# Moving the weights' buffers by 192 bytes in SBUF, and another w_ada item on TensorE

## The chip, the cores and the metric

The kernel runs on one core of a Trainium2 chip, in float32 (float32r for the large products). The metric is the device time in microseconds (us) of one execution; lower is better. Engines are named as the profile names them: PE is TensorE's matmul, PEld its load of the stationary operand, DVE is VectorE, ACT ScalarE, POOL GpSimd, SP SyncE, which issues most DMAs.

## The reference, cut to what matters

One layer of a streaming encoder over 256 frames of 2048 channels: a modulation from the vector c, a token mixer (gated linear attention beside a short convolution), and a convolutional feed-forward part.

```python
mod = silu(c) @ w_ada + b_ada                      # 2048 -> 6 * 2048
sh1, sc1, g1, sh2, sc2, g2 = split(mod, 6)
h = rmsnorm(x, norm_g[0]) * (1 + sc1) + sh1
y = token_mixer(h, w_in, ...)                      # h @ w_in, then w_out_gla, w_out_conv, w_o
x = x + g1 * rmsnorm(y, norm_g[1])
h = rmsnorm(x, norm_g[2]) * (1 + sc2) + sh2
gate, up = split(h @ w_up, 2)                      # 2048 -> 2 * 5632
y = (gelu(causal_dwconv(gate)) * up) @ w_down      # 5632 -> 2048
x = x + g2 * rmsnorm(y, norm_g[3])
```

Every weight is read once from HBM; the weights are most of the 363 MB that the profile counts.

## The kernel before, in words

**Three products for one.** The kernel splits each large operand into a float32r part and the rest: weights into `whi` and `wlo`, activations into a high and a low part. A product is the sum of high x high, high x low and low x high, three matmuls of float32r.

**A stream of chunks.** All weights pass as chunks of two blocks of 128 rows by 512 columns. For a chunk, SP issues a DMA into a buffer of the tag `raw` (nine buffers), ACT casts it into `whi` (L283), DVE subtracts it into `wlo` (L292), four buffers each, and TensorE does its matmuls. One list, `stream`, holds the order of all chunks, and `pump` walks it: DMAs are issued up to 13 chunks ahead, splits 4 ahead. `Feat` chunks (L339) put the weights' block in the array as the stationary operand and stream 256 columns of activations past it; `Tok` chunks (L394) hold 128 frames of the activations and stream 512 columns of weights.

**The places in SBUF.** One pool gives every tag its buffers in the order in which the tags are first named, so the size of one tile moves all tags behind it. The tile `H` holds the activations' two parts, 16 rows of `H_ROW` = 576 floats: the low part in columns 0 to 255, the high part from column 256 (with two more columns at one point). A row is 2304 bytes, nine times 256. Adding up the sizes, a tile's start modulo 256 bytes, its place, is

| tags | place |
|---|---|
| activations: `H` (all rows, both parts), `B`, `g8` | 64 |
| `t1` | 64 |
| `XF`, `t2` | 32 |
| `raw`, `c4`, `whi`, `wlo`, `A`, `cb` (behind `H`) | 0 |

Buffers of one tag and the blocks within them lie whole multiples of 256 bytes apart. Behind the 16 rows `H` has 32 unused floats.

**The start.** The first two of the six parts of the modulation (sh1, sc1) are needed before h exists. They are computed in five slices of channels (`SLICES`); the first covers 256 channels. For it w_ada comes in eight items, `Ada(0, 0)` to `Ada(0, 7)`, each two blocks of 128 rows in one `raw` buffer, two DMAs of 256 KB (L458). An item is added on DVE (L469 for the first block, L472 for the others: multiply by silu(c), add) or, if it stands in `ON_PE`, multiplied on TensorE (L229: the raw weights as stationary operand, one column of silu(c) streaming; a float32 matmul shows as two records). After the last item's turn DVE's sum is folded over partitions (L209 transposes, L211 adds) and `make_h` lets TensorE add the fold to the slice's bank (L217), from which DVE and ACT make scale and shift (L248, L249) and the first columns of H (L254 and following). The first L339 matmul needs these and the first `whi`.

```python
def split(self):                       # of Ada
    for t in range(self.nk):
        if (s, self.i) in ON_PE:
            break
        ...                            # one addition on DVE
    if self.last:
        acc_s[s] = fold(...)
def mm(self):
    if (s, self.i) in ON_PE:
        for t in range(self.nk):
            sum_cols(s, self.raw[:, :, t, :], sil[:, self.k0 + t:self.k0 + t + 1])
    if self.last:
        ...                            # make_h(s)
```

TensorE takes its work in the order of the stream, item by item.

Of the kernel before, what the change touches and what calls it, by code (L numbers as in the profile page):

```python
# [9 lines left out]
F32R = mybir.dt.float32r  # L10
# [5 lines left out]
P = 128  # L16
T = 256
D = 2048
KD = D // P
H = 4  # L20
# [7 lines left out]
TAU = 16.0  # L28
KT = 2
H_ROW = 576  # L30
NC = 512


# [21 lines left out]
MID0, MID = 2, 4  # L55
SQ0, SQ1 = 3, 4
EARLY_G = [1, 0, 6, 13]
ON_PE = {(0, 5)}


@with_exitstack
def hybrid_layer(ctx, tc, x, c, w_ada, b_ada, norm_g, w_in, w_a2, b_a2, gla_norm_g,
# [7 lines left out]
    def sb(shape, tag, bufs=1, dt=F32):  # L70
        count[0] += 1
        return pool.tile(list(shape), dt, tag=tag, bufs=bufs, name=f"{tag}_{count[0]}")
# [98 lines left out]
    for s in range(2):  # L171
        for q in range(2):
            ps = mm_banks()
            for a in range(8):
                k = 8 * q + a
# [13 lines left out]

    def moving():  # L190

        t = sb([P, KD * H_ROW + 32], "H", 1, F32R)[:, 0:KD * H_ROW].rearrange("p (k n) -> p k n", k=KD)
        return t[:, :, T:], t[:, :, 0:T]

    h_hi, h_lo = moving()
    mod1 = sb([P, 2, KD], "mod1")
    bmod1 = sb([P, 2, KD], "bmod1")
# [66 lines left out]
    class Chunk:  # L264
# [9 lines left out]
        def dma(self):  # L274
            g = self.g
            self.raw = sb([P, KT, NC], "raw", RAW_BUFS)[:, 0:self.n, :]
            r = g.row0 + self.k0 * P
            nc.sync.dma_start(
                self.raw, g.w[r:r + self.n * P, g.n0:g.n0 + NC].rearrange("(t p) n -> p t n", p=P))

        def split(self):
            self.hi = sb([P, KT, NC], "whi", SPLIT_BUFS, F32R)[:, 0:self.n, :]
            nc.scalar.copy(self.hi, self.raw)  # L283
            self.lo = sb([P, KT, NC], "wlo", SPLIT_BUFS, F32R)[:, 0:self.n, :]
            if pos[2] < first_w:
                first_lo.append(self.split_lo)
            else:
                self.split_lo()
# [154 lines left out]
    class Ada:  # L443
# [17 lines left out]
        def split(self):  # L461
            s = self.s
# [3 lines that stand above are left out]
# [14 lines left out]
        def mm(self):  # L480
            s = self.s
            if (s, self.i) in ON_PE:
                for t in range(self.nk):
# [322 lines left out]
    def post_ya(g):  # L806
        def post(j, v):
            if not m_t:
                m_t["hi"], m_t["lo"] = moving()
            k = 4 * g + j  # L810
            t = tiles(t2())
            nc.vector.tensor_mul(t, v, ga_t["t"][:, k:k + 2, :])
            nc.vector.tensor_add(t, t, gb_t["t"][:, k:k + 2, :])
            split_pair(m_t["hi"][:, k:k + 2, 0:T], m_t["lo"][:, k:k + 2, :], t)
        return post
# [326 lines left out]
    with tc.high_priority():  # L1142
        xs["hi"], xs["lo"] = moving()
        nc.vector.tensor_copy(xs["hi"][:, :, T], sh2)
        nc.vector.tensor_sub(xs["hi"][:, :, T + 1], sh2, f(xs["hi"][:, :, T]))
        for q in range(4):
            n = slice(512 * q, 512 * (q + 1))
            for s in range(2):
                def x1():
                    return nc.vector.scalar_tensor_tensor(  # L1150
                        xin["t"][:, s, n], y_t["t"][:, s, n], r1[:, s:s + 1], xin["t"][:, s, n],
                        op0=ALU.mult, op1=ALU.add).ins
                if len(mid) == 3:
                    with tc.issue_after(mid[2]):
                        x1()
                else:
                    ins = x1()
                    if s == 1:
                        mid.append(ins)
            for k in range(4 * q, 4 * q + 4, 2):  # L1160
                ps = sm_bank()
                for a in range(2):
                    for s in range(2):
                        nc.tensor.transpose(ps[:, a * T + s * P:a * T + (s + 1) * P],  # L1164
                                            xin["t"][:, s, (k + a) * P:(k + a + 1) * P], ident)
                for a in range(2):
                    sc, v = s2[:, k + a:k + a + 1], ps[:, a * T:(a + 1) * T]
                    hi = xs["hi"][:, k + a, 0:T]
                    mid_act.append(nc.scalar.mul(hi, v, sc).ins)
                    nc.vector.scalar_tensor_tensor(xs["lo"][:, k + a, :], v, sc, f(hi),  # L1170
                                                   op0=ALU.mult, op1=ALU.subtract)
# [63 lines left out]
```

## Time and profile before

| | |
|---|---|
| median of 3 runs | 1451.68 us (1450.31 to 1453.68) |
| the profiled execution | 1453.29 us |
| its span, first to last instruction | 1451.5 us |
| mean granted clock of TensorE | 0.994 |
| busy: PE, PEld, DVE, ACT | 98%, 92%, 71%, 55% |
| HBM read | 363.18 MB, 252 GB/s over the span |

The profile shows one execution. A row of the costliest groups reads: line, engine, operation, output <- inputs, their shapes, count, then busy time in us, mean duration in ns, and the engine's idle time ahead of it with what ended it. Matmuls overlap in the pipeline, so their duration (about 280 ns) is not what one costs; the distance of their starts is. A row of the chain or of the timeline begins with start and length in us. Tile names stand without their numbers (`t` for t1 and t2, `c` for c4, `g` for g8).

### The profile page before, as it was taken

How to read it: one execution, taken by the hardware profiler on the slowest of the kernel's cores; microseconds unless marked ns; L12 is line 12 of the kernel's file. 1: busy time of each engine (PE TensorE's matmuls, PEld its weight loads, DVE VectorE, ACT ScalarE, POOL GpSimd, SP SyncE). 2: the span in 40 equal slices, each digit the busy share in tenths (PEclk: the TensorE clock that was granted, in tenths of full speed). 3: DMA queues.
4: the chain of work that ended last, by engine and by line, in shares of the span. 5: the costliest groups of instructions: out<-in, count | busy, mean ns of one | idle time of the engine just before them, and what ended most of it. 6: DMA issues, size and time to landing. Idle time of an engine off the chain costs nothing.

```text
span 1451.5 us, 25558 instructions
## 1 busy us (share of the span) xinstructions
PE 1425.8 (98%) x10385; PEld 1336.3 (92%) x10385; DVE 1036.6 (71%) x1153; ACT 792.9 (55%) x952; POOL 7.1 (0%) x28
## 2 busy tenths in 40 slices
PE   6999999999999999999999999999999999999997
PEld 6999999899999999887999998789999988999986
DVE  6887878889988877975897666656666644555554
ACT  5788777689554655444764444344444433444443
POOL 0000000000000000000000000000000000000000
PEclk9999999999999999999999999999999999999999
DMA  9999989989988778886568777677776666666651
GB/s 353 366 339 310 375 286 360 328 288 331 372 285 280 245 251 317 304 299 183 151 199 264 238 234 235 231 239 236 230 228 204 200 188 190 187 184 185 186 174 59
DMA packets 178095, 366.97 MB, mean 253 GB/s; under 512 B 14026, under 2 KB 26648, under 8 KB 177209
## 3 DMA queue, kind: packets, MB, share of 16 engines
q1 hardware_dynamic: 176857, 362.17, 75.4%
q0 software_dynamic: 544, 2.11, 0.4%
q8 instruction: 81, 1.33, 0.4%
q10 hardware_dynamic: 576, 1.05, 0.2%
q14 instruction: 37, 0.30, 0.1%
HBM read 363.18 MB, written 2.11 MB: 252 GB/s over the span
## 4 chain that ended last, share of the span: by engine, by line
PE 93%; DVE 3%; DMA 2%; ACT 1%; issue 1%; SPq 0%; DVEq 0%; ACTq 0%
PE mm L339 63%; PE mm L394 28%; DMA raw<-in_w_ada_dram 2%; DMA XF<-in_x_dram 1%; DVE wlo L292 0%; DVE c L432 0%; DMA raw<-in_w_in_dram 0%; PE sm L1164 0%; SPq L458 0%; ACT whi L283 0%; DVE t L789 0%; PE sm L773 0%; DVE fold L211 0%; DVE c L472 0%; PE sm L217 0%
## 5 line engine op out<-in xcount | busy, mean ns | idle before, releaser
L283 ACT CAST whi<-raw 128x1024 fp32r<-128x1024 f32 (+1 forms) x503 | 512.6, 1024 | 525.3 <-PE mm L339 280.4
L292 DVE TENSOR_TENSOR wlo<-raw,whi 128x1024 fp32r<-128x1024 f32 (+1 forms) x503 | 595.4, 1191 | 285.5 <-ACT whi L283 275.7
L339 PE MATMUL mm<-H,whi 128*128 128x256 f32 (+1 forms) x4992 | 649.3, 281 | 1.6 <-ACT H L254 1.2
L339 PEld LDWEIGHTS mm<-H,whi 128*128 128x128 f32 x4992 | 616.1, 189 | 3.9 <-ACT H L254 1.3
L339 PE MATMUL mm<-H,wlo 128*128 128x256 f32 (+1 forms) x2496 | 350.2, 280 | 0.0
L339 PEld LDWEIGHTS mm<-H,wlo 128*128 128x128 f32 x2496 | 318.5, 188 | 0.0
L394 PE MATMUL mm<-whi,g 128*128 128x512 f32 x704 | 181.5, 395 | 0.0
L394 PEld LDWEIGHTS mm<-whi,g 128*128 128x128 f32 x704 | 131.9, 188 | 31.7
L432 DVE SCALAR_TENSOR_TENSOR c<-raw,sil,c 128x1024 f32<-128x1024 f32 x90 | 115.2, 1280 | 35.7 <-DMA raw<-in_w_ada_dram 35.6
L394 PE MATMUL mm<-whi,H 128*128 128x512 f32 x448 | 118.5, 396 | 0.0
L394 PEld LDWEIGHTS mm<-whi,H 128*128 128x128 f32 x448 | 83.5, 188 | 19.6
L394 PE MATMUL mm<-wlo,g 128*128 128x512 f32 x352 | 99.3, 395 | 0.0
L394 PEld LDWEIGHTS mm<-wlo,g 128*128 128x128 f32 x352 | 66.1, 188 | 16.0
L472 DVE SCALAR_TENSOR_TENSOR c<-raw,sil,c 128x768 f32<-128x768 f32 (+2 forms) x73 | 78.6, 1077 | 2.0 <-DMA raw<-in_w_ada_dram 1.4
L394 PE MATMUL mm<-wlo,H 128*128 128x512 f32 x224 | 65.7, 395 | 0.0
L432 DVE SCALAR_TENSOR_TENSOR cb<-raw,sil,cb 128x1024 f32<-128x1024 f32 x30 | 38.5, 1284 | 24.7 <-DMA raw<-in_w_ada_dram 24.7
L394 PEld LDWEIGHTS mm<-wlo,H 128*128 128x128 f32 x224 | 42.1, 188 | 10.2
L982 DVE SCALAR_TENSOR_TENSOR t<-mm,fcol,t 128x255 f32<-128x255 f32 x80 | 38.4, 480 | 1.2
L339 PE MATMUL mm<-B,whi 128*128 128x256 f32 x256 | 33.5, 282 | 0.0
L339 PE MATMUL mm<-g,whi 128*128 128x256 f32 x256 | 32.8, 280 | 0.0
L339 PEld LDWEIGHTS mm<-B,whi 128*128 128x128 f32 x256 | 31.4, 188 | 1.4 <-ACT t L712 0.8
L339 PEld LDWEIGHTS mm<-g,whi 128*128 128x128 f32 x256 | 31.3, 188 | 0.0
(193 smaller groups left out, 687.1 us busy)
## 6 DMA issues: line engine op xcount, KB each, us to landing
raw<-in_w_up_dram SPq DMA_DIRECT2D x176, 512.0 KB, 4.3
raw<-in_w_ada_dram SPq DMA_DIRECT2D x160, 512.0 KB, 5.2
raw<-in_w_in_dram SPq DMA_DIRECT2D x145, 512.0 KB, 5.8
raw<-in_w_down_dram SPq DMA_DIRECT2D x88, 512.0 KB, 3.8
raw<-in_w_o_dram SPq DMA_DIRECT2D x32, 512.0 KB, 5.6
raw<-in_w_ada_dram SPq DMA_DIRECT2D x32, 384.0 KB, 6.1
raw<-in_w_out_conv_dram SPq DMA_DIRECT2D x16, 512.0 KB, 6.1
raw<-in_w_out_gla_dram SPq DMA_DIRECT2D x16, 512.0 KB, 5.4
```

Of the source, the lines that this page charges most:

```text
L283: nc.scalar.copy(self.hi, self.raw)
L292: nc.vector.tensor_sub(self.lo, self.raw, f(self.hi))
L339: nc.tensor.matmul(dst[:, 0:cols], w[:, t, j * P:(j + 1) * P], m(ch.k0 + t, cols), start=first_in_bank and t == 0 and i == 0, stop=end and ...
L394: nc.tensor.matmul(self.out[s], m(c.k0 + t, T)[:, s * P:(s + 1) * P], w[:, t, :], start=first and t == 0 and i == 0, stop=end and t == c.n ...
L432: nc.vector.scalar_tensor_tensor(a, self.raw, sil[:, self.k:self.k + 1], a, op0=ALU.mult, op1=ALU.add)
L472: nc.vector.scalar_tensor_tensor(a, raw, sc, a, op0=ALU.mult, op1=ALU.add)
L982: nc.vector.scalar_tensor_tensor(dst[:, a, i:], v[:, a, 0:T - i], w(2 - i, a), dst[:, a, i:], op0=ALU.mult, op1=ALU.add)
```

## The change

Two edits. `H` is allocated with 80 unused floats instead of 32 behind its rows, and its use still begins at its first float (`H_AT` = 0). All tags behind it move by 192 bytes, so that `raw`, `c4`, `whi`, `wlo`, `A` and `cb` begin at place 192 of 256; `H`, `B` and `g8` stay at 64. And of the first slice's items TensorE takes the last, number 7, instead of number 5; DVE adds items 0 to 6.

```diff
 H_ROW = 576
+H_AT, H_PAD = 0, 80
 NC = 512
...
-ON_PE = {(0, 5)}
+ON_PE = {(0, 7)}
...
     def moving():
 
-        t = sb([P, KD * H_ROW + 32], "H", 1, F32R)[:, 0:KD * H_ROW].rearrange("p (k n) -> p k n", k=KD)
+        t = sb([P, KD * H_ROW + H_PAD], "H", 1, F32R)[:, H_AT:H_AT + KD * H_ROW]
+        t = t.rearrange("p (k n) -> p k n", k=KD)
         return t[:, :, T:], t[:, :, 0:T]
```

## Prediction

> **What bounds the kernel now.** I read the page's busy times and slices first, then the chain of waits, then short windows, because the change moves operands of nearly every matmul and I wanted the matmul's rhythm stage by stage.
>
> ```profile
> span 1451.5 us, 25558 instructions
> PE 1425.8 (98%) x10385; PEld 1336.3 (92%) x10385; DVE 1036.6 (71%) x1153; ACT 792.9 (55%) x952; POOL 7.1 (0%) x28
> PE   6999999999999999999999999999999999999997
> PE 93%; DVE 3%; DMA 2%; ACT 1%; issue 1%; SPq 0%; DVEq 0%; ACTq 0%
> L283 ACT CAST whi<-raw 128x1024 fp32r<-128x1024 f32 (+1 forms) x503 | 512.6, 1024 | 525.3 <-PE mm L339 280.4
> ```
>
> TensorE is busy from the second slice to the last, holds 93% of the chain that ended last, and the cast that makes whi waits mostly for TensorE to give a buffer back. So TensorE sets the pace and the others follow it. What a matmul costs from start to start is read off the chain's long uninterrupted pieces:
>
> ```profile
> 763.66 115.81 PE mm L339 x981
> 969.44 144.16 PE mm L339 x1224
> 1150.72 89.60 PE mm L394 x384
> 1240.32 135.68 PE mm L339 x1152
> ```
>
> With a moving operand of 256 columns (L339) that is 144.16 / 1224 = 117.8 ns, and 135.68 / 1152 = 117.8 ns; with 512 columns (L394) 89.60 / 384 = 233.3 ns. The piece of 981 gives 118.1. These are constant over stages with different loads on DVE, ACT and the DMAs.
>
> ```profile
> L339 PE MATMUL mm<-H,whi 128*128 128x256 f32 (+1 forms) x4992 | 649.3, 281 | 1.6 <-ACT H L254 1.2
> L339 PE MATMUL mm<-H,wlo 128*128 128x256 f32 (+1 forms) x2496 | 350.2, 280 | 0.0
> L339 PE MATMUL mm<-B,whi 128*128 128x256 f32 x256 | 33.5, 282 | 0.0
> L339 PE MATMUL mm<-g,whi 128*128 128x256 f32 x256 | 32.8, 280 | 0.0
> L394 PE MATMUL mm<-whi,g 128*128 128x512 f32 x704 | 181.5, 395 | 0.0
> L394 PE MATMUL mm<-whi,H 128*128 128x512 f32 x448 | 118.5, 396 | 0.0
> L394 PE MATMUL mm<-wlo,g 128*128 128x512 f32 x352 | 99.3, 395 | 0.0
> L394 PE MATMUL mm<-wlo,H 128*128 128x512 f32 x224 | 65.7, 395 | 0.0
> ```
>
> That is 8000 matmuls at 117.8 ns (942 us) and 1728 at 233.3 ns (403 us): 1345 of 1451.5 us hang on two rhythms. One nanosecond on the first is 8 us.
>
> **Edit 1, the places.** The longer H moves every tile named after it by 192 bytes: raw, c4, whi, wlo, A and cb from place 0 to 192 of 256. H, B and g8, the activations, stay at 64. No instruction and no byte of traffic is added. The question is whether the rhythm depends on the distance between the operand that streams and the one that is loaded, which goes from 64 to 128. No row of the trace has a whi or wlo at another distance, so its price is bounded.
>
> For an effect: there is a second rhythm at the same places.
>
> ```profile
> 25.00:31.00 6.00, 5.66 (x25) 5.47 (x26) 5.95 (x9) 3.61 (x5) 0.00 (x0) 0.50 1.06 399
> 68.40:70.90 2.50, 2.50 (x24) 2.50 (x23) 2.11 (x4) 2.50 (x6) 0.00 (x0) 1.00 0.94 329
> 744.00:763.00 19.00, 19.00 (x170) 19.00 (x170) 19.00 (x35) 12.65 (x17) 0.00 (x0) 1.00 0.65 187
> 800.00:850.00 50.00, 50.00 (x427) 50.00 (x426) 32.48 (x34) 22.18 (x26) 0.00 (x0) 1.00 0.75 237
> ```
>
> These are windows: start and end, length, then busy time and count of PE, PEld, DVE, ACT and POOL, granted clock, DMA share, GB/s. A matmul of 280 ns overlaps its neighbours, so a window counts 280 / 117.8 = 2.4 too many. From 800 to 850 that is 50.00 / (427 - 2.4) = 117.8 ns. From 744 to 763 it is 19.00 / (170 - 2.4) = 113.4 ns, at full clock, with the same operands, and with DVE fully busy. So up to 4.4 ns of the 117.8 are a matter of how streams meet in time.
>
> Against an effect: the weights' load is not what costs them.
>
> ```profile
> 397.82 0.19 PEld L339 LDWEIGHTS mm<-B,wlo 128*128 128x128 f32 x1
> 397.94 0.11 PEld L694 LDWEIGHTS sm<-H,t 128*32 128x32 f32 x1
> 398.05 0.28 PE L694 MATMUL sm<-H,t 128*32 128x256 f32 x1
> 398.99 0.28 PE L339 MATMUL mm<-B,whi 128*128 128x256 f32 x1
> ```
>
> Between 398.05 and 398.99 stand eight matmuls with weights of only 32 or 16 columns (tile t, place 32 or 160, so at distances that whi never has). Their load takes 0.11 us instead of 0.19, and yet they come every 0.94 / 8 = 117.5 ns. A quarter or an eighth of the weights read, at other distances, and the rhythm is the same. Also, during one L339 matmul the moving operand runs through 256 columns of 4 bytes while 128 columns of weights are read: 1024 against 512 bytes. The distance between the two therefore sweeps 512 bytes, two whole turns of 256, wherever it starts; in L394 it is 2048 against 512. A start at 128 instead of 64 changes when they meet, not how often. And 512 columns cost 233.3 / 117.8 = 1.98 times 256, although only one load of weights lies beside either: the cost goes with the moving columns. I take 0 for edit 1, by the L694 rows, which are the nearest to another distance; the ends are the quick rhythm everywhere and, by symmetry, the same 4.4 ns lost.
>
> The DMAs now write raw at place 192, where a row of 2 KB touches nine blocks of 256 bytes instead of eight.
>
> ```profile
> 4.00:9.00 5.00, 0.00 (x0) 0.00 (x0) 0.00 (x0) 3.13 (x6) 0.00 (x0) 1.00 1.00 399
> 25.00:62.00 37.00, 36.66 (x251) 34.88 (x252) 32.97 (x35) 25.27 (x27) 0.00 (x0) 0.91 1.05 393
> 100.00:300.00 200.00, 199.92 (x1524) 189.94 (x1523) 162.92 (x160) 151.76 (x172) 0.00 (x0) 1.00 0.94 331
> ```
>
> From 4 to 9 us the traffic is mostly x into XF, which lies at place 32: 399 GB/s at a share of 1.00. From 25 to 62 raw is written at place 0: 393 GB/s at 1.05. A destination off the 256-byte line is no slower, so I count nothing. The cover, if it were, is the 6% that the share of 0.94 between 100 and 300 us leaves; the other end of the price is rival E.
>
> **Edit 2, item 7 on TensorE.** Of the first slice's eight items DVE adds seven and TensorE one, before and after. Only which one changes.
>
> ```profile
> 13.86 5.26 DMA raw<-in_w_ada_dram
> ...
> 14.42 3.90 DVE L472 SCALAR_TENSOR_TENSOR c<-raw,sil,c 128x512 f32<-128x512 f32 x5 [0.15 <-DMA raw<-in_w_ada_dram]
> 19.21 3.12 DVE L472 SCALAR_TENSOR_TENSOR c<-raw,sil,c 128x512 f32<-128x512 f32 x4 [0.88 <-DMA raw<-in_w_ada_dram]
> 20.05 1.84 PE L229 MATMUL sm<-sil,raw 128*128 128x1 f32 x16
> 22.36 0.71 DVE L209 STREAM_TRANSPOSE raw<-c 128x512 f32<-128x512 f32 x1
> 22.48 1.04 ACT L283 CAST whi<-raw 128x1024 fp32r<-128x1024 f32 x1 [1.64 <-DMA raw<-in_w_in_dram]
> 23.10 0.69 DVE L211 TENSOR_REDUCE fold<-raw 128x16 f32<-128x512 f32 x1
> 23.84 0.25 PE L217 MATMUL sm<-fold,sel 128*32 128x4 f32 x8 [1.95 <-DVE fold L211]
> 25.34 4.09 PE L339 MATMUL mm<-H,whi 128*128 128x256 f32 x16 [1.25 <-ACT H L254]
> ```
>
> Now DVE runs dry at 14.42 + 3.90 = 18.32, waits 0.88 us until item 6 lands at 13.86 + 5.26 = 19.12, adds items 6 and 7 (3.12 us, to 22.33), folds, and TensorE starts the products at 25.34. After the change its last four additions are items 5 and 6. Item 5 is two and one transfers ahead of the one that lands at 19.12, each 256 KB, or 0.67 us at 393 GB/s: at 17.8 and 18.45. Item 6's second half lands at 19.8. So DVE goes on at about 18.4 and ends near 18.4 + 3.12 = 21.5, and the fold moves forward by about 0.85 us. TensorE's sixteen L229 matmuls (1.84 us) now wait for item 7, about 20.45 and 21.1; the second half ends near 21.1 + 0.92 = 22.0, under the fold, which ends at 23.8 - 0.85 = 22.95. That cover is 0.9 us; if item 7 landed later than that, the products would start later by the excess. L217 stands behind them in TensorE's queue, then H's scaling, then L339 at 24.5. The first cast, 22.48 + 1.04 = 23.52, is still in time. On SP's queue no DMA is moved; the buffer of item 5 comes free about 2 us earlier and that of item 7 about as now, behind a DMA share of 1.05 that cannot use it. Later casts wait for TensorE, so the 0.85 us is carried to the end.
>
> Sum: 0 - 0.85 = -0.85 us. The profiled execution took 1453.29 us with a span of 1451.5; the median of the runs is 1451.68. Set on the median: 1450.8 us. A difference of 0.2% (2.9 us) is about what a measurement of this kernel can tell from none.
>
> **The rivals.**
>
> A. The distance does count, and TensorE falls into the quick rhythm throughout. For it: 744 to 763. Against it: L694. 8000 x 4.4 ns = 35 us; for the 1728 of 512 columns between nothing and the same 3.7% (8.7 ns, 15 us). That gives 1451 - 0.9 - 35 to 50 = 1400 to 1415. ACT and DVE (55% and 71% busy) have room; the loads at 0.94 just have. [...]
>
> B. The quick rhythm takes some stages only, since it is entered after a pause and lost at the next (68.40 to 70.90, 744 to 763). 19 us of it now save 0.7 us; a tenth to all but a fifth of the stages would give 1415 to 1447.
>
> C. The stretch at half clock goes. From 25 to 31 us the clock is 0.50 and 25 matmuls take 6 us, after a pause from 20.05 + 1.84 = 21.9 to 25.3 with only L217 in it; the pause becomes 22.0 to 24.5. At 117.8 ns the 25 would take 3 us, so up to 3 us more: 1448. [...]
>
> D. The other side: at 128 apart the streams settle in a slower rhythm. Its place is L339, its price 8 us for each ns; the symmetrical 4.4 ns give 1486, half of it 1468. It decides from 0.5 ns on (117.8 to 118.3). For it: nothing holds 117.8 as a worst case, and the piece of 981 shows 118.1 on average. Against it: L694.
>
> E. Every block of 256 bytes that a packet touches costs the same. Then loads take 9/8 of their time, the share of 0.94 becomes 1.06, and TensorE waits for loads over the first 300 us: 0.06 x 300 = 18 us, 1469. Against it: 399 GB/s into XF. [...]
>
> **How the numbers follow.** Forecast (no change of rhythm, start earlier): 0.38. A 0.17, B 0.15, C 0.08, D 0.18, E 0.04. Faster by over 0.2%: A, B and most of C and a little of the forecast, 0.40. Same: 0.36. Slower: D, E and a little of the forecast, 0.24. The forecast's own range is 1448 to 1454. For 8 in 10 half of A (below 1405) and the upper parts of D and E (above 1468) are left out: 1405 to 1468.
>
> **What would show it.** Right: the chain's long pieces still at 117.8 and 233.3 ns; L217 about 0.85 us earlier, no DVE wait of 0.88 before the last four additions, L229 ending before the fold. Wrong: a window such as 800 to 850 with 443 matmuls (113.4) or with under 425; L229 ending after the fold; a clock of 1.00 from 25 to 31; times to landing of raw that grow. The prediction fails as a whole if the rhythm moves by more than 0.4 ns, since everything else is under 4 us.

## The result, and the profile after

The changed kernel takes 1462.61 us (median, 1461.16 to 1466.39) against 1452.68 us for the kernel before in the same comparison: a ratio of 1.0083, 95% interval 1.0065 to 1.0101. It is slower by 0.8%, where the prediction had 1450.8 us. What came is rival D, the slower rhythm, at about a third of the price that it was given.

From the page of the kernel after, and from its chain of waits (start, length, engine, tile, line, count; all lines of the kernel after stand two higher, so that L339 is L341 and L394 is L396):

```profile
span 1459.5 us, 25560 instructions
PE 1434.5 (98%) x10385; PEld 1347.0 (92%) x10385; DVE 1036.6 (71%) x1153; ACT 792.7 (54%) x952; POOL 7.1 (0%) x28
```

```profile
25.98 27.92 PE mm L341 x216
...
600.76 75.29 PE mm L396 x324
...
719.52 162.60 PE mm L341 x1368
882.12 52.99 PE mm L396 x228
...
971.87 146.88 PE mm L341 x1224
...
1156.16 89.22 PE mm L396 x384
1245.38 138.24 PE mm L341 x1152
1383.62 67.22 PE mm L396 x288
```

The same chain of the kernel before, where the prediction did not show it:

```profile
597.40 75.60 PE mm L394 x324
...
718.31 44.74 PE mm L339 x384
...
879.47 53.20 PE mm L394 x228
...
1376.00 67.22 PE mm L394 x288
```

DVE, ACT and the loads do the same work; TensorE alone is longer. The piece of 1224 matmuls grew from 144.16 to 146.88 us, from 117.8 to 120.0 ns each; the one of 1152 to 138.24 / 1152 = 120.0; the one of 1368 to 162.60 / 1368 = 118.9. With 512 columns the piece of 384 became shorter, 89.22 / 384 = 232.3 ns instead of 233.3, and the one of 288 stayed. So the price has a sign for each width: from start to start, over all stretches without a pause, the mean went from 117.67 to 119.21 ns for 256 columns and from 233.34 to 232.62 for 512. These means hide steps: nearly every stage of 256 columns in the kernel after stands at 118.7 or at 120.0 ns.

Along the chain, the end of the last product moved from 1443.22 (1376.00 + 67.22) to 1450.84, by 7.62 us: 0.64 at the start (25.34 to 25.98), 2.41 from there to the end of the piece of 324 (673.00 to 676.05), -1.84 in the norm between the two parts (to 718.31 and 719.52), and 6.41 from there on. By the rhythms it should be more: 8000 x 1.54 ns - 1728 x 0.72 ns = 11.1 us, and 0.64 for the start. So some 4 us are missing. One part of them is the clock, shown by windows of the kernel before and of the one after (columns as in the prediction; the clock is the third number from the end):

```profile
690.00:697.00 7.00, 6.47 (x28) 5.85 (x29) 6.41 (x12) 5.11 (x12) 0.00 (x0) 0.52 0.13 48
```

```profile
693.00:700.00 7.00, 6.10 (x44) 5.28 (x45) 7.00 (x14) 6.18 (x15) 0.00 (x0) 1.00 0.11 43
...
25.00:31.00 6.00, 5.02 (x25) 4.83 (x26) 5.81 (x11) 3.92 (x5) 0.00 (x0) 0.57 1.06 379
25.00:62.00 37.00, 36.02 (x252) 34.29 (x253) 33.42 (x37) 25.43 (x27) 0.00 (x0) 0.93 1.06 381
100.00:300.00 200.00, 199.95 (x1516) 190.39 (x1515) 161.84 (x159) 151.38 (x171) 0.00 (x0) 1.00 0.95 331
...
800.00:850.00 50.00, 50.00 (x424) 50.00 (x423) 32.31 (x34) 21.94 (x26) 0.00 (x0) 1.00 0.75 239
1000.00:1100.00 100.00, 100.00 (x836) 100.00 (x835) 66.16 (x72) 46.38 (x55) 0.00 (x0) 1.00 0.73 226
```

In the norm the profiled execution of before ran at a clock of 0.52, the one after at 1.00: up to 1.84 us that belong to the single execution (a second execution of the kernel before has 0.75 from 690 to 695 us, where the first has 0.53; one execution of the kernel with the places alone shows 0.68 from 695 to 700). The first L341 piece, of 216, is 0.74 us shorter (28.66 to 27.92) because less of it runs at half clock: from 30 to 31 us the clock is 0.50 before and 0.93 after, from 31 to 32 us 0.72 and 1.00. Of the 1.5 us that are left, about half lies between 400 and 535 us: that part became 0.77 us longer, where its 954 matmuls by 1.54 ns would give 1.5; TensorE waits for small steps there, and part of a slower rhythm can hide in the waits (from 400 to 535 us it is not busy for 0.62 us in the kernel before and for 0.19 in the one after). The remainder is not placed. The span grew by 8.0 us, the median by 9.9.

The window that the prediction named as a sign has 424 matmuls from 800 to 850 us, where 427 stood before; from 1000 to 1100 us it is 100.00 / (836 - 2.4) = 120.0 ns.

The start, from the timeline of the kernel after (start, length, engine, line; in brackets the idle time ahead and what ended it):

```profile
15.00 6.27 DVE L474 SCALAR_TENSOR_TENSOR c<-raw,sil,c 128x512 f32<-128x512 f32 x8 [0.28 <-DMA raw<-in_w_ada_dram]
...
20.97 1.95 PE L231 MATMUL sm<-sil,raw 128*128 128x1 f32 x16
...
22.96 0.71 DVE L211 STREAM_TRANSPOSE raw<-c 128x512 f32<-128x512 f32 x1 [1.69 <-PE sm L231]
...
24.44 0.29 PE L219 MATMUL sm<-fold,sel 128*32 128x4 f32 x8 [1.52 <-DVE fold L213]
25.98 3.24 PE L341 MATMUL mm<-H,whi 128*128 128x256 f32 x12 [1.25 <-ACT H L256]
```

DVE's additions now end at 21.27 instead of 22.33, without the wait of 0.88. And then DVE stands for 1.69 us, until TensorE has finished with item 7 at 22.92. The fold begins at 22.96, 0.60 later than before.

### The profile page after: what moved, and what is told of

It reads as the page before. It is cut to its first block, busy times and chain, and to the rows that moved or that the text cites. A ratio compares the mean times of both kernels' runs of the same rounds, so it can differ in the third digit from the quotient of the medians.

```text
span 1459.5 us, 25560 instructions
## 1 busy us (share of the span) xinstructions
PE 1434.5 (98%) x10385; PEld 1347.0 (92%) x10385; DVE 1036.6 (71%) x1153; ACT 792.7 (54%) x952; POOL 7.1 (0%) x28
## 4 chain that ended last, share of the span: by engine, by line
PE 97%; DVE 1%; DMA 1%; ACT 0%; SPq 0%; issue 0%; DVEq 0%; ACTq 0%
PE mm L341 67%; PE mm L396 28%; PE mm L177 1%; PE sm L775 0%; DMA raw<-in_w_ada_dram 0%; DMA raw<-in_w_in_dram 0%; PE mm L754 0%; PE sm L1166 0%; ACT whi L285 0%; DVE XF L1152 0%; PE sm L219 0%; PE sm L787 0%; DVE g L1070 0%; DVE wlo L294 0%; PE sm L231 0%
## 5 line engine op out<-in xcount | busy, mean ns | idle before, releaser
L285 ACT CAST whi<-raw 128x1024 fp32r<-128x1024 f32 (+1 forms) x503 | 512.5, 1024 | 547.7 <-PE mm L341 287.8
L341 PE MATMUL mm<-H,whi 128*128 128x256 f32 (+1 forms) x4992 | 655.6, 283 | 1.6 <-ACT H L256 1.2
L341 PEld LDWEIGHTS mm<-H,whi 128*128 128x128 f32 x4992 | 621.8, 189 | 4.0 <-ACT H L256 1.3
L341 PE MATMUL mm<-H,wlo 128*128 128x256 f32 (+1 forms) x2496 | 353.7, 282 | 0.0
L341 PEld LDWEIGHTS mm<-H,wlo 128*128 128x128 f32 x2496 | 321.4, 189 | 0.0
L396 PE MATMUL mm<-whi,g 128*128 128x512 f32 x704 | 181.2, 395 | 0.0
L396 PEld LDWEIGHTS mm<-whi,g 128*128 128x128 f32 x704 | 132.2, 188 | 31.1
L434 DVE SCALAR_TENSOR_TENSOR c<-raw,sil,c 128x1024 f32<-128x1024 f32 x90 | 115.0, 1278 | 36.9 <-DMA raw<-in_w_ada_dram 36.8
L396 PE MATMUL mm<-whi,H 128*128 128x512 f32 x448 | 118.1, 395 | 0.0
L396 PEld LDWEIGHTS mm<-whi,H 128*128 128x128 f32 x448 | 83.7, 188 | 18.9
L396 PE MATMUL mm<-wlo,g 128*128 128x512 f32 x352 | 99.1, 395 | 0.0
L396 PEld LDWEIGHTS mm<-wlo,g 128*128 128x128 f32 x352 | 66.2, 188 | 15.7
L396 PE MATMUL mm<-wlo,H 128*128 128x512 f32 x224 | 65.5, 395 | 0.0
L396 PEld LDWEIGHTS mm<-wlo,H 128*128 128x128 f32 x224 | 42.2, 188 | 9.8
L341 PE MATMUL mm<-B,whi 128*128 128x256 f32 x256 | 33.9, 285 | 0.0
L341 PE MATMUL mm<-g,whi 128*128 128x256 f32 x256 | 33.1, 282 | 0.0
L341 PEld LDWEIGHTS mm<-B,whi 128*128 128x128 f32 x256 | 31.8, 189 | 1.3 <-ACT t L714 0.8
L341 PEld LDWEIGHTS mm<-g,whi 128*128 128x128 f32 x256 | 31.5, 188 | 0.0
```

The source lines that it names most:

```text
L341: nc.tensor.matmul(dst[:, 0:cols], w[:, t, j * P:(j + 1) * P], m(ch.k0 + t, cols), start=first_in_bank and t == 0 and i == 0, stop=end and ...
L396: nc.tensor.matmul(self.out[s], m(c.k0 + t, T)[:, s * P:(s + 1) * P], w[:, t, :], start=first and t == 0 and i == 0, stop=end and t == c.n ...
L434: nc.vector.scalar_tensor_tensor(a, self.raw, sil[:, self.k:self.k + 1], a, op0=ALU.mult, op1=ALU.add)
```

## The experiments

### One edit at a time

```diff
 # the second edit alone, on the kernel before
-ON_PE = {(0, 5)}
+ON_PE = {(0, 7)}
```

> Before, with item 7 instead of item 5 on TensorE; the places stay as before. Theory (the places set the rhythm, and the fold's scratch takes the buffer of item 7, so that DVE's fold waits for TensorE): the first L339 matmul about 0.6 us later than in the kernel before, a wait of DVE's fold for TensorE of over 1 us, the rhythms unchanged at 117.8 and 233.3 ns, time +0.3 to +1 us (ratio 1.0002 to 1.0007). Rival (the order of the start sets the phase in which all later matmuls run): rhythms of 118.7 and 120.0 ns as in the changed kernel, time +8 to +10 us.

```diff
 # the first edit alone: the changed kernel with
-ON_PE = {(0, 7)}
+ON_PE = {(0, 5)}
```

> Before, with the weights at place 192 (80 unused floats); item 5 stays on TensorE. Theory (the places set the rhythm): 256 columns at 118.7 or 120.0 ns by stage, 512 columns at 232.4 or 233.3 ns, start as before, time +7 to +9 us. Rival (the start sets the phase): 117.8 and 233.3 ns, time within 1 us of before.

The item alone: 1450.67 us against 1452.11, ratio 0.9990 (0.9975 to 1.0005), no difference. The places alone: 1463.63 us, ratio 1.0075 (1.0054 to 1.0096). From the chain with the places alone:

```profile
974.55 146.88 PE mm L341 x1224
...
1158.85 89.22 PE mm L396 x384
```

To the hundredth these are the pieces of the kernel after. Edit 1 carries all of the loss. The timeline of the item alone shows the late start by itself:

```profile
22.78 0.71 DVE L209 STREAM_TRANSPOSE raw<-c 128x512 f32<-128x512 f32 x1 [1.46 <-PE sm L229]
...
25.80 3.46 PE L339 MATMUL mm<-H,whi 128*128 128x256 f32 x13 [1.25 <-ACT H L254]
```

The first product is 0.46 us later, which the median can't tell.

### The distance, or the weights' own place

```diff
 # the places alone, with H moved as well
-H_AT, H_PAD = 0, 80
+H_AT, H_PAD = 48, 80
```

H lies at place 0 here and the weights at 192, so that the weights are 64 below H again, modulo 256, as before; B and g8 stay 128 from the weights.

> As the run with the places only, but H begins 48 floats into its tile, so that H lies at place 0 and the weights at 192: 64 apart, as before; B and g8 stay at 64, 128 from the weights. Item 5 on TensorE. Theory (the distance of the two operands counts, modulo 256): H's matmuls back at 117.8 ns, those with B or g8 at 118.7 or 120.0, and 512 columns with H at 233.3, with g8 at 232.4; time +1 to +2 us. Rival (the weights' own place counts): 118.7 or 120.0 ns for H too, time +7 to +9 us.

1452.97 us, ratio 1.0002 (0.9986 to 1.0018). From its chain:

```profile
968.51 144.16 PE mm L341 x1224
...
1149.79 89.23 PE mm L396 x384
```

The products with H are back at 117.8 ns, and those of 512 columns with g8, still 128 away, stay at 89.23 / 384 = 232.4. One kernel shows both rhythms by the operand's distance. The weights' own place is refuted as a cause, and with it the loads into it.

### The fold's scratch

The fold transposes into a buffer of the tag `raw`. Item 7's buffer is the one that it gets, so it has to wait until item 7 has been read, now by TensorE.

```diff
 # the item alone, with the first slice's fold in a buffer of t2
-        tr = sb([P, CW], "raw", RAW_BUFS)[:, 0:n]
+        tr = (t2() if own else sb([P, CW], "raw", RAW_BUFS))[:, 0:n]
 ...
-                    acc_s[s] = fold(acc_s[s].rearrange("p j n -> p (j n)"))
+                    acc_s[s] = fold(acc_s[s].rearrange("p j n -> p (j n)"), own=s == 0)
```

> Before, with item 7 on TensorE and the first slice's fold transposed into a buffer of the tag t2 instead of raw. Theory (the fold waited for TensorE only through the buffer): the wait of the fold for TensorE is gone, L217 about 0.85 us earlier than before, the first L339 matmul at about 24.5 us instead of 25.3, time -0.5 to -1 us. Rival (the fold isn't what the start waits for, DMA landings are): first L339 within 0.2 us of before.

```profile
21.40 0.71 DVE L209 STREAM_TRANSPOSE t<-c 128x512 f32<-128x512 f32 x1
...
22.89 0.25 PE L217 MATMUL sm<-fold,sel 128*32 128x4 f32 x8 [0.30 <-DVE fold L211]
25.81 3.37 PE L339 MATMUL mm<-H,whi 128*128 128x256 f32 x15 [2.67 <-ACT whi L283]
```

The wait is gone and L217 comes 0.95 us earlier than before, so the buffer was the cause. But the first product does not come earlier: ACT has made H first (1.09 us from 23.73) and the cast of the first whi stands behind it (0.94 us), and TensorE waits 2.67 us for that cast. In all 1457.48 us, ratio 1.0037 (1.0022 to 1.0052), slower: two more waits for ACT follow, 2.05 us for a cast to whi near 55 and 2.54 us for H near 72. That the changed order on ACT brings them was not tested. The expectation was missed: behind the wait that was removed stood the first cast.

### All distances in steps of 32 bytes

Only the unused floats behind H differ in these kernels (the rest as in the kernel before, with item 5 on TensorE).

```diff
-H_AT, H_PAD = 0, 80
+H_AT, H_PAD = 0, 40     # weights at place 32; 48: 64; 56: 96; 64: 128; 72: 160; 88: 224
```

> As the run with the places only, with 40 unused floats: weights at place 32, 32 below the activations. If the streams meet in blocks of 64 bytes, this is as place 0 (before): 117.8 and 233.3 ns, time within 2 us of before. If the distance counts byte by byte, a rhythm of its own, between that of place 0 and that of place 64.

> With 48 unused floats: weights at place 64, the same as the activations, distance 0. If the farther the better, or the nearer the worse, this is the slowest place of all, over 120 ns and over 1464 us. If 128 is the worst (as 118.7 to 120.0 ns at 128 against 117.8 at 64 suggests), distance 0 is at or below 117.8 ns, time at or below before.

> With 56 unused floats: weights at place 96, 32 above the activations. Blocks of 64 bytes: as place 64. Byte by byte: a rhythm between those of places 64 and 128.

> With 64 unused floats: weights at place 128, 64 above the activations instead of 64 below. If only how far the two are apart counts, 117.8 and 233.3 ns as before, and a time within 2 us of before. If the sign counts, 256 columns take another rhythm than 117.8 ns (the one that 512 columns have the other way round stays unknown), time off by over 4 us.

> 72 floats behind H: the weights at 160, 96 ahead of H. It stands between 64 ahead (113.36 and 228.9 ns) and 128 (119.2 and 232.6). Theory, a smooth dependence on the distance: about 116 and 231 ns, 1440 us. Rival, each distance has its own short pattern with no order in it (0: 120.0, 32: 118.3, 64: 113.4): anything from 113 to 120 ns, 1420 to 1462.

> 88 floats behind H: the weights at 224, 96 behind H. It stands between 128 (119.2 and 232.6 ns) and 64 behind (117.78 and 233.33). Smooth: about 118.5 and 233 ns, 1457 us. Rival, no order: 113 to 120 ns, 1420 to 1462.

One long piece of each width from each chain, in the order of the places 32, 64, 96, 128, 160, 224:

```profile
965.91 142.81 PE mm L341 x1224
...
1145.50 89.59 PE mm L396 x384
```

```profile
973.47 146.87 PE mm L341 x1224
...
1158.15 87.07 PE mm L396 x384
```

```profile
974.77 144.84 PE mm L341 x1224
...
1156.90 89.60 PE mm L396 x384
```

```profile
952.25 138.74 PE mm L341 x1224
...
1126.74 87.89 PE mm L396 x384
```

```profile
970.32 143.62 PE mm L341 x1224
...
1151.34 89.59 PE mm L396 x384
```

```profile
979.76 146.88 PE mm L341 x1224
...
1164.44 89.95 PE mm L396 x384
```

The rows in order of the distance, weights' place less H's, in bytes modulo 256; the last one is the changed kernel, with item 7 on TensorE, all others have item 5. The rhythms are means from start to start over all stretches without a pause; the fourth column is 8000 and 1728 times their difference to before.

| distance | 256 columns, ns | 512 columns, ns | by the rhythms, us | span, us (less 1451.5) | ratio of the medians (95%) |
|---|---|---|---|---|---|
| -96 (place 224) | 119.98 | 234.24 | +20.1 | +17.0 | 1.0132 (1.0106 to 1.0158) |
| -64 (before) | 117.67 | 233.34 | 0 | 0 | 1 |
| -32 (place 32) | 116.72 | 233.29 | -7.7 | -6.3 | 0.9979 (0.9968 to 0.9990) |
| 0 (place 64) | 119.97 | 226.88 | +7.3 | +6.0 | 1.0057 (1.0035 to 1.0079) |
| 32 (place 96) | 118.33 | 233.32 | +5.3 | +6.8 | 1.0057 (1.0037 to 1.0077) |
| 64 (place 128) | 114.01 | 228.91 | -36.9 | -31.9 | 0.9822 (0.9792 to 0.9851) |
| 96 (place 160) | 117.96 | 233.37 | +2.4 | +1.7 | 1.0031 (1.0019 to 1.0043) |
| 128 (after, place 192) | 119.21 | 232.62 | +11.1 | +8.0 | 1.0083 (1.0065 to 1.0101) |

The spans follow the rhythms with the right sign everywhere and within 5 us. The dependence on the distance isn't smooth: 64 is the best for 256 columns and its neighbours 32 and 96 are 4 ns slower. The sign counts: -64 and 64 are 32 us apart. And the widths go their own ways: at 0 the one of 256 columns is at its slowest, 120.0 ns, and the one of 512 at its quickest, 87.07 / 384 = 226.7 ns.

In all these kernels raw, c4, A and cb move together with whi and wlo, so a collision of TensorE's reads with the accesses of other engines would go with the place as well. The traces speak against it. From 800 us on, the matmuls of 256 columns during which ACT and DVE are both idle start as far apart as those during which both are busy: 120.00 and 120.00 ns at place 64 (316 and 383 matmuls), 113.38 and 113.34 at place 128 (175 and 460). And at place 64 the products of 512 columns come 68 in 15 us with a DMA share of 0.60 (1390 to 1405 us) and also with one of 0.01 (1420 to 1435). For 256 columns the loads were not separated in this way.

### Distance alone, modulo 256

```diff
 # H at place 0, weights at 64: 64 above H, as at place 128
+H_AT, H_PAD = 48, 48
 # and, apart from that, no unused floats: weights at 128, every address 256 bytes lower
+H_AT, H_PAD = 0, 0
```

> H at place 0, the weights at 64: again 64 ahead of H, as where 113.36 ns was seen, but no operand of H's products is at a place that it had there; B and g8 stay at 64, so that they lie 0 from the weights. Theory, the signed distance modulo 256 alone sets the rhythm: H's matmuls at 113.3 ns (256 columns) and 228.9 (512), those of B and g8 at 120.0 and 226.8, as at distance 0 before; with the 7488 at 256 columns of H 33 us shorter and the 512 at 256 columns of B and g8 1 us longer, about 1425 us. Rival, place 128 of the weights is what was quick: then 64 is as it was with H at 64 (120.0 ns), about 1459. Rival, both places count: anything else.

> No unused floats behind H: the weights at place 128 again, but every address behind H is 256 bytes lower than in the run with 64 floats. Theory, only the distance modulo 256 counts: the same 113.3 and 228.9 ns, about 1424 us. Rival, the pattern repeats over 512 bytes or more (or the absolute address counts): another rhythm of those seen, 117.8 (1452) to 120.0 ns (1459).

The first took 1434.47 us, ratio 0.9883 (0.9858 to 0.9908), the second 1425.27, ratio 0.9815 (0.9785 to 0.9845). The chain of the first:

```profile
755.81 111.46 PE mm L341 x981
...
919.14 35.59 PE mm L396 x156
954.73 144.16 PE mm L341 x1224
...
1136.01 87.08 PE mm L396 x384
```

With every operand of H's products at another place than in the kernel with place 128, the quick rhythm is there again (111.46 / 981 = 113.6 ns with the transition, 113.34 without), and the products with g8, at distance 0, run at 226.8 ns as at place 64. That is the distance theory. But some stages between the g8 products run at 144.16 / 1224 = 117.8 ns, the rhythm of -64, and that makes the 9 us by which the expectation was missed. The second kernel shows the quick pieces of place 128 at all large stages from 700 us on (138.74 us for the 1224 and 87.89 for the 384, as there), so with every address 256 bytes lower the rhythms came again; two stages before 270 us were at 117.8 (56.26 us for the 476, 63.09 for the 534, as in the kernel before).

### What decides between 113.3 and 117.8 ns

> The kernel with 64 floats behind H once more, nothing changed. Theory, which of the two rhythms (113.3 or 117.8 ns) a stage of several waves takes is fixed by the program: the same stages quick as in its first profile, span within 1 us of 1419.6. Rival, it is taken anew in each execution: some stages of 50 to 140 us change sides, by 2 to 5 us each.

> The kernel before once more. Fixed by the program: the quick rhythm from 743.8 to 763.1 us alone, as in its first profile, span 1451.5. Taken anew: another stretch at 113.3 ns, or none; each 100 us of it saves 3.8 us.

The chain of the second execution of the kernel with place 128 has

```profile
588.37 75.60 PE mm L396 x324
```

where its first had

```profile
587.90 74.16 PE mm L396 x324
```

and the second execution of the kernel before has

```profile
130.12 54.15 PE mm L339 x476
...
714.41 161.38 PE mm L339 x1368
```

where the first had 56.26 us for the 476 and its quick 19 us at 744. Its span is 1448.2 against 1451.5 us. So at 64 in either direction two rhythms are possible for 256 columns, 113.3 and 117.8 ns, and some stages take now one and now the other in executions of the same program. Not all do. With place 128 the two executions differ in the first 120 us and between 520 and 660, and from 707 us on their pieces agree to within 0.02 us, with 256 columns at 113.3 ns nearly throughout; their spans are 1419.6 and 1419.4 us. So neither expectation holds for all stages.

At -64 the quick rhythm is rarer: it took 170 to some 900 of 7800 matmuls, and every stage of 512 columns stood at 233.3 in all profiles of that distance with H. At 64 with item 5, 512 columns mostly run at 228.9 behind a quick stage and at 233.3 behind one of 117.8 (571 to 588 at 117.8, then the 588.37 piece at 75.60 / 324 = 233.3); a short stage of 36, near 53 us in the first execution, stands at 229.5 behind one of 117.8. The three times that a quick stage ran straight into 512 columns at -64 (near 184 us in the second execution of the kernel before and in the run with H moved, near 190 us in the one with the fold in t2), the stage behind was at 117.8; at 64 it stayed quick each time. So it fits that at -64 the 512 columns throw TensorE out of the quick rhythm; that is read from the profiles, and not tested by itself. Most other changes of rhythm fall at a break of 0.2 us or more, or at a few small matmuls of another line. Not all do: in the kernel before, the quick rhythm begins near 743 us, in the middle of the unbroken piece of 384 that the chain shows from 718.31 to 763.05. What decides it there stays open.

### Both together

```diff
-H_AT, H_PAD = 0, 80
+H_AT, H_PAD = 0, 64     # the rest as in the changed kernel, item 7 on TensorE
```

> The weights at 128 (64 floats behind H) together with item 7 on TensorE. Theory, the two edits are independent and item 7 is worth nothing: 113.3 ns in most stages, 1424 us, give or take the stages that fall to 117.8 (up to 4 us). Rival, the start decides which of the two rhythms each stage takes: a changed start gives another set of quick stages, 1420 to 1450 us.

1421.42 us against 1451.29, ratio 0.9795 (0.9776 to 0.9813); the kernel with place 128 and item 5, compared at the same time, 1420.46, ratio 0.9783 (0.9767 to 0.9799). The item is worth nothing here either. The version that beats both kernels is the one with 64 unused floats, or with none: 2% faster than before, nearly 3% faster than the change.

## Why the prediction was wrong

**What bounds.** Right, and it is why the result is what it is: 1345 us on two rhythms, 8 us for each ns.

**Edit 1, "I take 0 for edit 1, by the L694 rows".** This step failed. It measured +1.54 ns and -0.72 ns, 11.1 us by the rhythms and some 10 us in the median. Two arguments stood behind it.

The L694 rows showed 117.5 ns for other weights at other distances. Those distances, tile t at places 32 and 160 with H at 64, are -32 and 96. For whi itself these turned out to be 116.7 and 118.0 ns, both within one nanosecond of before. The two samples happened to be ones that can't tell what 128 does, and a row of eight is short: with 120.0 ns all around, the same rows still came every 117.6 to 117.8 ns at place 64 and, from one row of eight to the next, every 114.9 to 118.3 at place 224.

The two whole turns (1024 against 512 bytes, "when they meet, not how often") were an argument, not a measurement. At eight distances the same instructions gave means from 114.0 to 120.0 ns. The symmetry used for the other end ("by symmetry, the same 4.4 ns lost") was too wide: the slowest of all distances is 120.0 ns, 2.2 above 117.8. The prediction asked only whether the distance goes from 64 to 128; it dropped the sign, and the sign is worth 32 us.

The window from 744 to 763 had said that 4.4 ns hang on how the streams meet. It was right to price rivals A and D by it, and wrong to let eight matmuls outweigh it. It belonged to the quick of two rhythms at -64; it said nothing of 128.

With every instruction the same, the place of the weights moved the matmul of 256 columns from 113.3 ns (place 128) to 120.0 (place 64). By what way, no run shows.

**Edit 2, "That cover is 0.9 us".** The first half was right: DVE ends at 21.27, forecast 21.5, and the 0.88 wait is gone; L229 ends at 22.92, forecast 22.0. The step that failed took the fold to be independent of L229. It writes into item 7's buffer, so there is no cover: the start came 0.64 us later instead of 0.85 earlier. And with the cover made (the fold in t2) the first cast was late next, against "the first cast is still in time". The edit is worth nothing by either way: 0.9990 and 1.0037.

**The rivals.** A: the quick rhythm exists, at 64 the other way round; its 1400 to 1415 us was near the 1420 that it gives there. B: the change of rhythm by stage is real, and most changes fall at a short break, as B had it; but after the change the two rhythms were 118.7 and 120.0 ns, no quick one among them, and the one near 743 us in the kernel before came without a break. C: the pause became 25.98 - 22.92 = 3.1 us instead of 2.5, and from 25 to 31 us the clock was 0.57, so the stretch did not go; that a shorter pause would bring the full clock was an estimate, and no run shows which length would. D came, at 1.54 ns where 2.2 and 4.4 were named; its point of decision, 0.5 ns, was passed. E: one price for every block was a supposition, and no run bears it out: the share from 100 to 300 us is 0.95 against 0.94, at 331 GB/s both times, so nine blocks do not cost 9/8. The table confirms it: place 128 is off the 256-byte line as well, and is the fastest.

## What to carry to other kernels

Where TensorE is busy throughout and its matmuls take one rhythm for hundreds of us, the place of the stationary operand relative to the moving one, modulo 256 bytes, is a parameter worth a scan (the medians of the eight distances spread over some 3% here, 1424 to 1470 us), and a change of any tile's size can move it by accident. The long pieces of the chain, divided by their counts, show it at once. Before an addition is moved to another engine, look whose buffer the next step will write to: a scratch tile from a shared tag waits for the last reader of what it replaces (the fold 1.69 us here).

## What of the hardware was not expected

- The rhythm of a float32r matmul of 256 columns was 113.3, 116.7, 117.3, 117.8, 118.3, 118.7 or 120.0 ns at full clock; of 512 columns 226.7, 228.9, 232.4, 233.3 or 234.2. Which of them came went with the distance modulo 256 bytes: 120.0 alone at -96 and 0, 118.3 at 32, mostly 116.7 at -32; 113.3 and 117.8 at -64 and 64, 118.7 and 120.0 at 128, and 117.3, 118.7 and 120.0 at 96. Why these, no run tells.
- At a distance of 64 or -64 the same program took its two rhythms partly in other stages from one execution to the next: 3 us of span between two executions of the kernel before.
- Behind a pause of 2.43 us (to 690.05 us in the kernel before, to 693.03 in the one after) the half clock came in some executions and not in others (0.52 and 1.00), worth up to 1.8 us.
- Loads into raw from 25 to 62 us moved 391 to 399 GB/s with raw at place 0 (three executions) and 372 to 382 at all other places (thirteen), at the same share of 1.04 to 1.06: perhaps a small price, some 3%, of a destination off the 256-byte line. Between 100 and 300 us nothing of it is left (331 to 334 GB/s in the same three, 329 to 341 in the thirteen), and with the fold in t2, where TensorE waits more, it was 368 at place 0; so the cause stays open.
